# Head logits of depth 64 in a two-block transformer kernel: zero-padded queries over 128 partitions in place of products over half of the partitions

## The chip, the cores and the metric

The kernel runs on one core of one Trainium2 chip, as one launch. The metric is the device time of a launch in microseconds. Three runs of the kernel before the change took 1594.09, 1598.08 and 1592.15 us (median 1594.09). Times of single instructions below come from one profiled execution.

## The reference

The input is 256 tokens of 1024 features. Two blocks follow each other, each with two layers, all in float32.

- First block, per layer: RMS norm, one wide projection, then three mixers side by side: a gated delta rule with 4 heads, an MLA attention with 8 heads, and a gated linear recurrence. Their outputs are gated, joined and projected back.
- Second block, per layer: a feed-forward of 2816 hidden units, a mixer, a second feed-forward. The mixer joins a memory attention (4 heads of 64 dimensions over 256 memory tokens) with a recurrence (layer 0) or with a forgetting attention of 12 heads of 64 dimensions (layer 1, called fox).

Three attentions form logits with a depth of 64. In MLA a head's depth is 128 + 64: the 64 rotary dimensions of the query against one rotary key that all heads share.

```
qf = concat([q_nope (128), q_pe (64)]);  kf = concat([k_nope (128), k_pe (64, same for all heads)])
logits = einsum('bhqd,bhkd->bhqk', qf, kf) * 192**-0.5          # causal, 8 heads, both layers
logits = einsum('bhqd,bhkd->bhqk', rms(q), rms(k)) * 64**-0.5   # memory: 4 heads, both layers
logits = q.k / sqrt(64) + D_t - D_s                              # fox: 12 heads, causal, one layer
```

## The kernel before

Activations are kept with features on the 128 partitions and 256 tokens along a row. Weights stream from DRAM in chunks of 1 MB; ScalarE writes a rounded part `wh` of a chunk and VectorE the remainder `wl`, both in float32r. A linear layer is three TensorE products per 128 x 128 weight tile (`mm3`: high-high, high-low, low-high), with 256 columns each, into PSUM tiles called `acc` (4 banks). The attentions work in plain float32 with PSUM tiles called `mix` (4 banks). The trace shows two TensorE passes for every float32 product, and one for a float32r product; "pass" is used for one such MATMUL below.

Two heads of depth 64 share a tile of 128 partitions: the even head on partitions 0 to 63, the odd one on 64 to 127. The logits of a head multiply one half of the query tile with the same half of the key tile (`half = slice(64 * g, 64 * g + 64)`), so TensorE uses 64 of its rows:

- `mla_pair` (line 1243): per head g and block b of 128 queries, one product of depth 128 starts a PSUM group and the rotary product of depth 64 ends it: `matmul(ps[:, :n], qp[half, q], kpe[half, :n], start=False, stop=True)`. `kpe` holds the shared rotary key twice, on both halves. `qp` is formed from a PSUM tile: VectorE shuffles it and multiplies by the cosine, GpSimd multiplies the shuffled copy by the sine and adds both. The last of these, the GpSimd addition, releases the product. There are 4 pairs in each of two layers: 32 products, half of them with 128 key columns and half with 256.
- `mem_attn` (line 1470): `matmul(ps, q[half, g, t], self.km[l][half, g, :], start=True, stop=True)`, 8 products of 256 columns in each of two layers.
- `fox` (line 1678): the same form, 24 products, half with 128 and half with 256 columns.

`qheads` (line 1442) makes the queries of the last two: token-major projection, sums of squares per head, the scale `r` (a power on GpSimd), four transposes into one `mix` tile, and one ScalarE copy with the gain per feature (`features`). VectorE reads the logits from PSUM together with `r`.

The order of the instructions is not the written one. `trace` records every call; `Order.schedule` then simulates the five engines with nominal costs, lags and tile slots, and each engine in turn takes one of its ready instructions by urgency (the recording order for TensorE; for others the first TensorE instruction that needs them). `Order.issue` (line 543) emits the result, so every instruction of the trace stands under line 543. Each engine executes its list in order.

Of the kernel before, what the change touches and what calls it, by code (L numbers as in the profile page):

```python
# [13 lines left out]
ALU = mybir.AluOpType  # L14
# [7 lines left out]
FF = 22  # hidden tiles of a feed-forward  # L22
# tile sizes (columns of 4 bytes) and their slots
SLOTS = {"raw": (2048, 3), "wh": (1024, 3), "wl": (1024, 3), "s1": (256, 20), "s2": (512, 48), "s3": (384, 12),
         "col": (24, 56)}
# order of the 64 rope dimensions: partners lie 16 lanes apart in a quadrant of 32
# [3 lines left out]
# ---------------------------------------------------------------- host layout  # L30
# [3 lines left out]
def _pack(W, chunks):  # L34
    """(first k tile, k tiles, columns) -> flat; each chunk lies [128, k tiles, columns]"""
    out = []
    for k0, kt, cols in chunks:
        w = W[k0 * P:(k0 + kt) * P][:, cols]
        out.append(w.reshape(kt, P, -1).transpose(1, 0, 2).reshape(-1))
    return np.concatenate(out)  # L40
# [46 lines left out]
# order of the 8 tiles of 128 that the second block's output products sum over: four that are ready early, then the rest  # L87
# [27 lines left out]
def gu_pack(G, U):  # L115
    w = np.stack([G.reshape(8, P, FF, P), U.reshape(8, P, FF, P)], axis=3)  # [k, p, j, 2, f]
    return np.ascontiguousarray(w.transpose(2, 1, 0, 3, 4)).reshape(-1)
# [6 lines left out]
# columns of the parameter tile: name -> (offset, columns)  # L124
# [17 lines left out]
def prm_pack(i):  # L142
# [6 lines left out]
    def taps(w):  # [4, C] -> [128, C/128 * 4]  # L149
        return w.reshape(4, -1, P).transpose(2, 1, 0).reshape(P, -1)  # L150
# [33 lines left out]
# constants that depend on shapes alone  # L184
# [76 lines left out]
# ---------------------------------------------------------------- instruction order  # L261
# The kernel below is traced first; then each engine's instructions are put in an order that keeps the engines busy
# (a list scheduling over the traced dependences with the engines' nominal costs), and issued in that order.
ENG = ("tensor", "scalar", "vector", "gpsimd", "sync")
# how much later than the earliest of its ready instructions an engine may start a more urgent one
SLACK = {"tensor": 0.0, "scalar": 150.0, "vector": 40.0, "gpsimd": 100.0, "sync": 0.0}
PATIENCE = 400  # how far an instruction may fall behind its place in the tracing order
# free slots of a tag below which tiles are given out in tracing order only
RESERVE = {"s1": 6, "s2": 10, "s3": 4, "col": 16, "raw": 3, "wh": 3, "wl": 3, "mix": 2, "acc": 1}
# from the end of an instruction on one engine to the start of a dependent one on another  # L270
# [19 lines left out]
class Tracer:  # L290
    """stands for one engine: notes its instructions instead of issuing them"""
# [8 lines left out]
class Order:  # L300
# [10 lines left out]
    # ---- tracing  # L311
# [42 lines left out]
    def touch(self, op, r, w):  # L354
# [3 lines left out]
        if h is None:  # L358
            h = self.hist[name] = ([], [])  # writes, reads
            self.tile[name] = (t.tag, t.bufs or t.tag_meta.bufs)  # L360
            self.first.append(name)
            self.uses[name] = 0
# [66 lines left out]
    # ---- scheduling  # L429
    def schedule(self):  # L430
        """each engine in turn takes, among the instructions that could start within its slack, the first traced; tiles
        get slots in tracing order, or past it while more than the tag's reserve is free"""
# [8 lines left out]
        # urgency: the tracing order for TensorE; for the others, the first TensorE instruction that needs the result  # L441
# [104 lines left out]
# ---------------------------------------------------------------- kernel  # L546
class Kern:
    def __init__(self, ctx, tc, aps):
# [20 lines left out]
        # scratch in DRAM: blocks of the delta rule's triangles, their inverses (zero outside the diagonal blocks)  # L569
# [6 lines left out]
    def start(self):  # L576
        """the first loads in the order of their use, and TensorE kept busy meanwhile, so that its clock is up"""
# [39 lines left out]
    # ---- tiles: few sizes, so that a slot serves every stage  # L617
# [52 lines left out]
    # ---- weights: packed chunks streamed from DRAM in order, split exactly into two float32r parts  # L670
# [19 lines left out]
    def mm3(self, out, a, b, start, stop):  # L690
        """a: stationary parts, b: moving parts"""
# [16 lines left out]
    def unit(self, out, w, X, k0=0, first=True, last=True):  # L708
        """out[features, tokens] += w^T X over w's k tiles"""
# [5 lines left out]
    def proj(self, raw, X, sink):  # L715
        """the 128-column units of raw (one or two): sink(n, psum [128, n, 256])"""
# [6 lines left out]
    def proj_tok(self, raw, X, sink):  # L723
        """token-major: sink(token block, psum [128 tokens, columns])"""
# [17 lines left out]
    # ---- token statistics  # L742
# [4 lines left out]
    def colsum(self, ps, sq, rhs=None):  # L747
        """ps[:, b] = sum over partitions of sq[:, tokens of block b]"""
# [5 lines left out]
    def bcast(self, col):  # L754
        """col [128 tokens, 2] -> [128, 256], the same in every partition"""
# [13 lines left out]
    # ---- a stage's operand: the residual times its gain in float32r parts, sums of squares on the way  # L769
# [38 lines left out]
    def feed(self, j, ps, scale, stages):  # L808
        """x tile j += scale * ps, and on to the next stages"""
# [8 lines left out]
    # ---- feed-forward  # L818
# [26 lines left out]
    # ---- small pieces  # L845
# [6 lines left out]
    def silu2(self, ps, rb):  # L852
        """2 silu(ps * rb) for psum [128, n, 256]"""
# [8 lines left out]
    def softplus(self, x):  # L862
        """max(x, 0) + log1p(exp(-|x|)) for a few columns"""
# [7 lines left out]
        V.tensor_tensor(t[1], t[1], t[2], ALU.mult)      # z  # L871
        V.tensor_tensor(t[2], t[1], t[1], ALU.mult)      # z^2
# [12 lines left out]
    def conv(self, out, x, w, bias=None):  # L885
        """causal depthwise convolution of 4 taps along the tokens"""
# [8 lines left out]
    def softmax_t(self, z, mi, out):  # L895
        """z [128 queries, keys] = -logits, mi = their row minimum: out[key block] (psum) = P^T"""
# [10 lines left out]
    # ---- first block  # L907
    def gdn_scalars(self, l, raw, st):
        """rope key, write strength beta and log decay"""
# [27 lines left out]
    def gdn_proj(self, l, hp, kind, raw, st, gp):  # L937
        """keys, queries or values (kind 0, 1, 2) of heads 2hp, 2hp+1: convolution and 2 silu; sums of squares per token"""
# [25 lines left out]
    def gdn_rows(self, hp, gp, beta, gd):  # L964
        """rows k k^T and k q^T with the decays between their tokens: the diagonal blocks and the one beside them"""
# [52 lines left out]
    # DRAM scratch of 8 (head, block) squares of 128, the last rows padded so that all 16 x 16 diagonal blocks are equidistant  # L1018
# [6 lines left out]
    def gdn_inverse16(self):  # L1025
        """inverses of the 16 x 16 diagonal blocks (unit upper triangular) of four heads, one block a partition"""
        nc, V = self.nc, self.nc.vector

        def v(t, e, r, c):
            """the e x e blocks at (r, c) of the 2e x 2e diagonal blocks"""  # L1030
# [30 lines left out]
    def gdn_out(self, hp, gp):  # L1061
        """the rest of the inverses, values through the triangle, outputs [128 tokens, 2, 128] per head and their scales"""
# [3 lines left out]
        for h in range(2):  # L1066
            tu = self.s2((P, 2, 2, P))  # [block, T and its transpose U]
# [3 lines left out]
        for h in range(2):  # L1071
# [9 lines left out]
            need = [slice(0, 64), slice(64, 96)]  # T is needed there only  # L1081
# [55 lines left out]
    def rowsq(self, ps, out):  # L1137
        """out[:, b] = sums of squares of psum [128 tokens, 2 blocks of 128]"""
# [5 lines left out]
    def out_t(self, o, rr, gain, gate):  # L1144
        """token-major o [128, 2, 128] times its token scales, features first, times gain and gate, split"""
# [10 lines left out]
    def lru_pair(self, l, tp, raw, st, lw, hb):  # L1156
# [3 lines left out]
        def sink(n, ps):  # L1160
            xr = self.scaled(ps, st["rb"])
            for g in range(2):
# [8 lines left out]
                # twice the sigmoid, accurate where it is small: (1 + tanh |z/2|) exp(min(z, 0))  # L1171
# [11 lines left out]
        # -1 / (1 + t): (1 + e^-2x) / 2 and a Newton step  # L1183
# [9 lines left out]
    def mla_q(self, l, raw, st, mq, t0):  # L1193
        """tiles t0, ... of the query latent"""
# [12 lines left out]
    def mla_qr(self, mq, st):  # L1207
        """logits' scale per query: 192^-1/2 rsqrt(mean + eps / r^2), negated"""
# [22 lines left out]
    def lat_r(self, sq, n, st):  # L1231
        """rsqrt(mean + eps / r^2): the norm of a latent that still lacks its input's factor r"""
# [10 lines left out]
    def mla_pair(self, l, hp, raw, st, mq, rq, kvl, kpe, mixed):  # L1243
# [19 lines left out]
        G.tensor_tensor(qp, qp, sw, ALU.add)  # L1263
# [555 lines left out]
```

## Time and profile before

| | |
|---|---|
| timed runs | 1594.09 us median, 1592.15 to 1598.08 |
| span of the profiled execution | 1588.5 us, 5.6 us under the median; the page gives no other time of that execution |
| TensorE matmuls busy | 1569.5 us (99%), 12712 passes |
| VectorE, ScalarE, GpSimd busy | 1183.2 us (74%), 836.4 us (53%), 191.8 us (12%) |
| DMA | 46.9% of 16 engines' span |

A matmul's busy time in the trace includes time in the pipeline, so neighbouring passes overlap: a pass listed with 285 ns starts 120 ns after the one before it. What a pass costs is read from the distance of starts. In a merged row "x2" the start is that of its first instruction. A row names the rows and columns of the array as `64*128` (rows * columns) before the shape of the moving operand.

### The profile page before, as it was taken

The page shows a single profiled execution, that of the slowest core. Times are in us where ns is not written, and L with a number is a line of the kernel's source. Part 1 is how long each engine was busy: PE and PEld are TensorE (multiplying, and loading weights), DVE is VectorE, ACT ScalarE, POOL GpSimd, SP SyncE. Part 2 cuts the span into 40 slices and gives each one's busy share as a digit, 9 for nine tenths or more (in the row PEclk, how much of TensorE's full clock was granted, in tenths as well). Part 3 has the DMA queues.
Part 4 walks back from the last instruction along what each step waited for, and adds up shares of the span by engine and source line. Part 5 has one row for each costly group of instructions (what it writes and reads, how often), then busy time and mean ns, then how long its engine had stood idle before and what let it go on. Part 6 is the DMA issues. An engine that isn't in the chain of part 4 may idle for free.

```text
span 1588.5 us, 31207 instructions
## 1 busy us (share of the span) xinstructions
PE 1569.5 (99%) x12712; PEld 1520.3 (96%) x12712; DVE 1183.2 (74%) x2249; ACT 836.4 (53%) x1508; POOL 191.8 (12%) x196
## 2 busy tenths in 40 slices
PE   8999999999999999999999999999999999999999
PEld 8988999988989999999999999999999998999999
DVE  8987968996987677756888777665777666777753
ACT  5467745547765544445445444555444456654442
POOL 2301002311114100002102000021000321110000
PEclk9999999999999999999999999999999999999999
DMA  8343445343435455454334555544555743355553
GB/s 283 118 140 107 171 140 179 119 143 107 163 133 186 160 186 184 175 185 147 123 117 159 186 186 173 185 176 162 184 186 175 244 145 107 121 173 186 179 173 126
DMA packets 54598, 257.82 MB, mean 162 GB/s; under 512 B 11308, under 2 KB 21688, under 8 KB 27576
## 3 DMA queue, kind: packets, MB, share of 16 engines
q1 hardware_dynamic: 54456, 255.85, 46.9%
q8 instruction: 99, 1.62, 0.4%
q14 instruction: 43, 0.35, 0.1%
HBM read 252.39 MB, written 3.43 MB: 161 GB/s over the span
## 4 chain that ended last, share of the span: by engine, by line
PE 85%; DVE 8%; POOL 2%; issue 2%; ACT 1%; DMA 1%; SPq 0%; POOLq 0%; DVEq 0%; ACTq 0%
PE acc L543 74%; PE mix L543 11%; DVE s L543 5%; DVE wl L543 2%; POOL col L543 1%; POOL s L543 1%; DVE col L543 1%; ACT s L543 1%; ACT wh L543 0%; DMA s<-tri_out 0%; DMA tri_out<-s 0%; DMA prm<-in_prm_dram 0%; SPq L543 0%; DVE x L543 0%; ACT L543 0%
## 5 line engine op out<-in xcount | busy, mean ns | idle before, releaser
L543 PE MATMUL acc<-s,wh 128*128 128x256 f32 x6720 | 1237.5, 285 | 0.0
L543 PEld LDWEIGHTS acc<-s,wh 128*128 128x128 f32 x6720 | 1051.8, 192 | 6.9 <-issue 4.6
L543 PE MATMUL acc<-s,wl 128*128 128x256 f32 x3360 | 957.1, 285 | 1.0 <-DVE wl L543 1.0
L543 ACT ACTIVATE wh<-raw 128x1024 fp32r<-128x1024 f32 (+1 forms) x470 | 489.1, 1041 | 574.9 <-PE acc L543 410.2
L543 DVE TENSOR_TENSOR wl<-raw,wh 128x1024 fp32r<-128x1024 f32 (+1 forms) x470 | 571.4, 1216 | 241.2 <-ACT wh L543 238.8
L543 PEld LDWEIGHTS acc<-s,wl 128*128 128x128 f32 x3360 | 644.9, 192 | 2.4 <-DVE wl L543 1.4
L543 PE MATMUL mix<-s,s 128*128 128x128 f32 (+7 forms) x1072 | 162.4, 291 | 5.7 <-DVE col L543 2.4
L543 POOL TENSOR_TENSOR s<-s,s 128x256 f32<-128x256 f32 x75 | 92.8, 1240 | 597.4 <-ACT s L543 596.2
L543 PEld LDWEIGHTS mix<-s,s 128*128 128x128 f32 (+5 forms) x1072 | 119.0, 168 | 34.8 <-issue 9.1
L543 ACT ACTIVATE s<-s 128x256 fp32r<-128x256 f32 (+3 forms) x311 | 134.1, 439 | 27.0 <-DVE s L543 25.3
L543 DVE TENSOR_TENSOR s<-s,s 128x256 fp32r<-128x256 f32 (+6 forms) x302 | 128.8, 436 | 13.5 <-ACT s L543 8.1
L543 PE MATMUL acc<-wh,s 128*128 128x256 f32 x640 | 126.5, 290 | 0.0
L543 DVE TENSOR_TENSOR s<-acc,s 128x512 f32<-128x512 f32 (+1 forms) x134 | 91.9, 686 | 44.2 <-PE acc L543 43.1
L543 PEld LDWEIGHTS acc<-wh,s 128*128 128x128 f32 x640 | 103.7, 194 | 2.3 <-issue 1.6
L543 PE MATMUL acc<-wl,s 128*128 128x256 f32 x320 | 92.5, 289 | 0.0
L543 ACT ACTIVATE s<-mix 32x64 f32<-32x64 f32 (+6 forms) x208 | 65.2, 327 | 50.2 <-PE mix L543 47.5
L543 DVE SCALAR_TENSOR_TENSOR s<-s,s 128x256 f32<-128x256 f32 (+2 forms) x168 | 81.8, 493 | 5.0 <-ACT s L543 4.8
L543 POOL TENSOR_TENSOR col<-col,mhalf 128x2 f32<-128x2 f32 (+2 forms) x31 | 44.7, 1442 | 228.8 <-DVE col L543 228.8
L543 POOL TENSOR_TENSOR s<-s,cst 128x256 f32<-128x256 f32 x36 | 33.6, 946 | 311.9 <-DMA s<-rows 161.3
L543 PEld LDWEIGHTS acc<-wl,s 128*128 128x128 f32 x320 | 62.1, 194 | 1.0 <-issue 1.0
L543 DVE SCALAR_TENSOR_TENSOR x<-acc,x 128x256 f32<-128x256 f32 x96 | 39.7, 419 | 29.2 <-PE acc L543 29.1
L543 PE MATMUL mix<-cst,s 128*128 128x128 f32 (+2 forms) x338 | 57.2, 267 | 3.7 <-DVE s L543 1.7
(94 smaller groups left out, 733.0 us busy)
## 6 DMA issues: line engine op xcount, KB each, us to landing
raw<-in_gu_dram SPq DMA_DIRECT2D x88, 1024.0 KB, 4.8
raw<-in_win_dram SPq DMA_DIRECT2D x36, 1024.0 KB, 5.0
raw<-in_dn_dram SPq DMA_DIRECT2D x32, 1024.0 KB, 4.8
raw<-in_wo_dram SPq DMA_DIRECT2D x24, 1024.0 KB, 4.8
raw<-in_wina_dram SPq DMA_DIRECT2D x13, 1024.0 KB, 4.8
raw<-in_dn_dram SPq DMA_DIRECT2D x16, 768.0 KB, 4.2
raw<-in_winb_dram SPq DMA_DIRECT2D x7, 1024.0 KB, 4.8
raw<-in_wkv_dram SPq DMA_DIRECT2D x6, 1024.0 KB, 4.8
```

Of the source, the lines that this page charges most:

```text
L543: getattr(getattr(self.nc, op.eng), op.fn)(*op.args, **op.kw)
```

## The change

The three logits no longer cut the operands in halves. The query tile is stored twice, each copy with zeros in place of the other head, and the product runs over all 128 partitions. In `mla_pair` two VectorE multiplications by a 0/1 column (`hsel`, a constant that was there before) write the copies. In `qheads` the gain is multiplied by the same column, and the PSUM tile of the transposes is copied twice. `features` is cut in two for that. The file of the changed kernel also has comments and docstrings removed; the line numbers of `issue` stay.

```diff
@@ mla_pair
         G.tensor_tensor(qp, qp, sw, ALU.add)
+        qz = self.s2()
+        for g in range(2):
+            V.tensor_scalar(qz[:, g, :], qp, self.c("hsel")[:, g:g + 1], None, ALU.mult)
...
-            half = slice(64 * g, 64 * g + 64)
...
-                nc.tensor.matmul(ps[:, :n], qp[half, q], kpe[half, :n], start=False, stop=True)
+                nc.tensor.matmul(ps[:, :n], qz[:, g, q], kpe[:, :n], start=False, stop=True)
@@ qheads, features
-        q = self.s2()
-        self.features(q, qt, gain)
+        pt = self.features_ps(qt)
+        q = []
+        for h in range(2):
+            gh = self.col(1)
+            V.tensor_tensor(gh, gain, self.c("hsel")[:, h:h + 1], ALU.mult)
+            q.append(self.s2())
+            nc.scalar.activation(q[h], pt, AF.Copy, scale=gh)
         return q, r
@@ mem_attn
-                    nc.tensor.matmul(ps, q[half, g, t], self.km[l][half, g, :], start=True, stop=True)
+                    nc.tensor.matmul(ps, q[h][:, g, t], self.km[l][:, g, :], start=True, stop=True)
@@ fox
-                        nc.tensor.matmul(ps, q[half, g, b * P:(b + 1) * P], self.ksh[c][half, g, :n],
+                        nc.tensor.matmul(ps, q[h][:, g, b * P:(b + 1) * P], self.ksh[c][:, g, :n],
                                          start=True, stop=True)
```

The planner runs again over the whole program. Two places show what it makes of the MLA pairs. TensorE, third pair of the first layer, before: `mix_524`, `529`, `539`, `544` are the logits of (head 0, block 0), (0, 1), (1, 0), (1, 1); `s2_506` with `s2_505` are keys and queries of depth 128, `s1_184` is the rotary key and `s1_507` the rotary query.

```order
L543 MATMUL acc_522_600<-wh_517_595,s2_133_209 128x256
L543 MATMUL mix_524_602<-s2_506_584,s2_505_583 128x128 [waits Activation_49]
L543 MATMUL mix_524_602<-s1_184_260,s1_507_585 128x128 [waits Pool_49]
L543 MATMUL mix_529_607<-s2_506_584,s2_505_583 128x256
L543 MATMUL mix_529_607<-s1_184_260,s1_507_585 128x256
L543 MATMUL mix_539_617<-s2_506_584,s2_505_583 128x128
L543 MATMUL mix_539_617<-s1_184_260,s1_507_585 128x128
```

The same place after the change, where `mix_527`, `532`, `542` are the first three logits and `s2_518` is the tile of the two padded queries:

```order
L543 MATMUL acc_525_603<-wh_520_598,s2_133_209 128x256
L543 MATMUL mix_527_605<-s2_508_586,s2_507_585 128x128 [waits Activation_49]
L543 MATMUL mix_532_610<-s2_508_586,s2_507_585 128x256
L543 MATMUL mix_527_605<-s1_184_260,s2_518_596 128x128 [waits DVE_49]
L543 MATMUL mix_532_610<-s1_184_260,s2_518_596 128x256
L543 MATMUL mix_542_620<-s2_508_586,s2_507_585 128x128
L543 MATMUL mix_542_620<-s1_184_260,s2_518_596 128x128 [waits DVE_49]
```

The rotary product waits for VectorE where it waited for GpSimd, and the 256-column product of block 1 has moved in front of it. VectorE at the same place after the change; `s1_509` is the rotary query, which GpSimd completes between the second row and the fifth, and `wl` tiles are weight remainders:

```order
L543 STREAM_SHUFFLE s1_517_595<-acc_514_592 128x256 [waits PE_49]
L543 TENSOR_TENSOR s1_509_587<-acc_514_592,cst_66 128x256
L543 TENSOR_TENSOR wl_561_639<-raw_556_634,wh_560_638 128x1024 [waits Activation_49]
L543 SCALAR_TENSOR_TENSOR s1_485_563<-s2_320_398,s2_481_559 128x256
L543 TENSOR_SCALAR s2_518_596<-s1_509_587,cst_66 128x256 [waits Pool_49]
L543 TENSOR_SCALAR s2_518_596<-s1_509_587,cst_66 128x256
L543 SCALAR_TENSOR_TENSOR s2_493_571<-s2_494_572,s2_493_571 128x512
```

The two `TENSOR_SCALAR` rows are new in VectorE's list, and the first of them waits for GpSimd with the rest of the list behind it.

## Rows read from the trace of the kernel before

**Rows 1.** Page, part 1: busy time and share of the span by engine.
```profile
PE 1569.5 (99%) x12712; PEld 1520.3 (96%) x12712; DVE 1183.2 (74%) x2249; ACT 836.4 (53%) x1508; POOL 191.8 (12%) x196
```
**Rows 2.** Page, part 4: the chain that ended last, by engine.
```profile
PE 85%; DVE 8%; POOL 2%; issue 2%; ACT 1%; DMA 1%; SPq 0%; POOLq 0%; DVEq 0%; ACTq 0%
```
**Rows 3.** Groups of TensorE by shape: count | busy us, mean ns | idle before.
```profile
L543 PE MATMUL mix<-s,s 64*128 64x256 f32 x88 | 24.5, 426 | 2.4 <-DVE col L543 2.4
L543 PE MATMUL mix<-s,s 64*128 64x128 f32 x56 | 12.5, 329 | 2.7 <-POOL s L543 2.1 <-DVE s L543 0.5
```
**Rows 4.** TensorE in order of time, depth 128 only: start, duration, what, [idle before].
```profile
54.42 0.59 PE L543 MATMUL mix<-s 128*128 128x256 f32 x2
54.66 0.47 PE L543 MATMUL acc<-s,wl 128*128 128x256 f32 x1
54.97 0.40 PE L543 MATMUL acc<-s,wh 128*128 128x256 f32 x2
...
130.80 0.39 PE L543 MATMUL mix<-s,s 128*128 128x128 f32 x2
130.94 0.36 PE L543 MATMUL acc<-s,wh 128*128 128x256 f32 x1
131.15 0.28 PE L543 MATMUL acc<-s,wl 128*128 128x256 f32 x1
```
**Rows 5.** The same of an MLA pair with all sixteen logits passes in one run.
```profile
388.87 4.14 PE L543 MATMUL mix<-s,s 128*128 128x128 f32 x16
392.94 0.51 PE L543 MATMUL acc<-s,wh 128*128 128x256 f32 x2
393.28 0.29 PE L543 MATMUL acc<-s,wl 128*128 128x256 f32 x1
```
**Rows 6.** The same of the last third of fox: begin and end of its logits.
```profile
1362.22 0.28 PE L543 MATMUL acc<-s,wl 128*128 128x256 f32 x1
1362.43 0.93 PE L543 MATMUL mix<-s,s 64*128 64x128 f32 x8
...
1366.92 0.50 PE L543 MATMUL acc<-s,wh 128*128 128x256 f32 x2
1367.26 0.28 PE L543 MATMUL acc<-s,wl 128*128 128x256 f32 x1
```
**Rows 7.** The same of the memory attention, layer 0, and GpSimd's power there.
```profile
739.18 2.58 POOL L543 TENSOR_TENSOR col<-col,mhalf 128x8 f32<-128x8 f32 x1 [4.64 <-DVE col L543]
739.88 1.14 PE L543 MATMUL mix<-s,s 64*128 64x256 f32 x8
740.95 0.39 PE L543 MATMUL acc<-s,wh 128*128 128x256 f32 x1
742.66 1.97 PE L543 MATMUL mix<-s,s 64*128 64x256 f32 x8 [1.20 <-DVE col L543]
744.56 0.39 PE L543 MATMUL acc<-s,wh 128*128 128x256 f32 x1
```
**Rows 8.** GpSimd's rotary addition and the first rotary product in two pairs.
```profile
83.61 2.98 POOL L543 TENSOR_TENSOR s<-s,s 128x256 f32<-128x256 f32 x1
86.65 0.49 PE L543 MATMUL mix<-s,s 64*128 64x128 f32 x2 [1.12 <-POOL s L543]
...
438.02 1.59 POOL L543 TENSOR_TENSOR s<-s,s 128x256 f32<-128x256 f32 x1
439.66 5.43 PE L543 MATMUL mix<-s,s 64*128 64x128 f32 x14 [0.84 <-POOL s L543]
```
**Rows 9.** Groups nearest to what is added, and those that wait for weight remainders.
```profile
L543 DVE TENSOR_SCALAR s<-s,col 128x256 f32<-128x256 f32 x56 | 19.3, 359 | 0.2
L543 ACT ACTIVATE s<-mix,prm 128x512 f32<-128x512 f32 x10 | 6.8, 680 | 4.8 <-PE mix L543 4.8
L543 PE MATMUL acc<-s,wl 128*128 128x256 f32 x3360 | 957.1, 285 | 1.0 <-DVE wl L543 1.0
```
**Rows 10.** A stretch: length, busy (instructions) of PE, PEld, DVE, ACT, POOL, granted clock, DMA, GB/s.
```profile
441.50:448.30 6.80, 6.80 (x23) 5.05 (x24) 5.37 (x22) 3.60 (x13) 0.00 (x0) 0.50 0.66 251
```

More of the change, by code (lines that the diff above doesn't have):

```diff
@@ L1457, in qheads, with features_ps @@
         V.tensor_scalar(r, r, -0.125, None, ALU.mult)
-        q = self.s2()
-        self.features(q, qt, gain)
+        pt = self.features_ps(qt)
[5 more added lines that the diff above has]
+            nc.scalar.activation(q[h], pt, AF.Copy, scale=gh)
         return q, r
     def features(self, out, kt, gain):
+        self.nc.scalar.activation(out, self.features_ps(kt), AF.Copy, scale=gain)
+    def features_ps(self, kt):
         pt = self.mix().rearrange("p (g t) -> p g t", g=2)
@@ L1467, in features @@
                 self.transpose(pt[:, g, b * P:(b + 1) * P], kt[:, b, g * P:(g + 1) * P])
-        self.nc.scalar.activation(out, pt, AF.Copy, scale=gain)
+        return pt
     def mem_attn(self, l, raw, st, mixed):
@@ L1476, in mem_attn @@
             for h in range(2):
-                half = slice(64 * h, 64 * h + 64)
                 pt = self.mix().rearrange("p (k t) -> p k t", k=2)
@@ L1698, in fox @@
                 for h in range(2):
-                    half = slice(64 * h, 64 * h + 64)
                     m = self.fox_bias(2 * tl + h)
```

## The prediction

> **What bounds the kernel now.** I read the page's busy times first. TensorE is busy 99% of the span, VectorE 74%, ScalarE 53% [rows 1]. Busy overlaps between neighbouring passes, so this alone does not say that TensorE sets the end. The chain of waits does: 85% of it lies on TensorE and 8% on VectorE [rows 2]. So the question is what TensorE's list costs, pass by pass, and where it waits. The groups by shape give the passes that the change touches: 88 of 256 columns and 56 of 128 columns use 64 rows of the array [rows 3], that is 144 passes or 72 products. Their mean duration is modelled and cannot be used as a price. The price is read from the timeline, as distance between starts.
>
> **The price of a pass over all rows.** Take a run of float32 passes that `acc` passes follow, from its first start to the start of the second `acc` row. An `acc` pass takes 0.12 us: in [rows 5] the first two stand in one row at 392.94 and the third starts at 393.28, while the second starts 0.12 before the third, at 393.16. Two 256-column passes over 128 rows take 54.97 - 54.42 = 0.55 us, less 0.12 for the first `acc` pass leaves 0.43, so 0.215 each. Two 128-column passes take 131.15 - 130.80 = 0.35, less 0.12, so 0.115 each [rows 4].
>
> **The price of a pass over 64 rows.** The MLA pair of [rows 5] has 16 passes: eight of depth 128 and eight of depth 64, in turn, half with 128 and half with 256 columns. From 388.87 to 393.16 they take 4.29 us. Sixteen passes over 128 rows would take 8 x 0.215 + 8 x 0.115 + 0.12 = 2.76 us. The difference is 1.53 us for four products of depth 64, or 0.38 us each. No wait stands in these rows, so it is the array itself: a product over 64 rows between products over 128 rows loses time at its start, between its two passes and at its end.
>
> The places differ, so I price each.
>
> - MLA: 32 products of the kind of [rows 5], 32 x 0.38 = 12.2 us less.
> - Fox: [rows 6] runs from 1362.22 to the second `acc` pass at 1367.26 - 0.12 = 1367.14, 4.92 us. In it stand 8 `acc` passes (0.96 us) and the 16 passes of 8 products, half with 128 and half with 256 columns. At the prices over all rows this is 0.96 + 8 x 0.115 + 8 x 0.215 = 3.60 us. The difference is 1.32 us, and there are three such thirds: 4.0 us less. This is net: in the first run the two heads of a tile lie on different halves and run side by side, which is lost, but each later product stands alone between `acc` passes, which pays.
> - Memory attention: here the halves do run side by side. The first eight passes take 740.95 - 739.88 = 1.07 us to the first `acc` row [rows 7], against 7 x 0.215 + 0.03 = 1.53 us over all rows: about 0.5 us longer in each of two layers. What hides it is the wait behind it: TensorE stands 1.20 us until VectorE frees PSUM banks, and VectorE waits for the scale `r`, whose power ends on GpSimd at 739.18 + 2.58 = 741.76. None of that depends on the products. Without this cover it would cost 1.0 us. The second eight take 744.56 - 742.66 = 1.90 us to the first `acc` row against 1.53, 0.37 us longer; but banks that VectorE frees one by one may set the pace there. Bounds 0 and 0.4 us a layer; I take 0.15, nearer to zero since VectorE's reads are not shortened. 0.3 us less in both.
>
> Together 12.2 + 4.0 + 0.3 = 16.5 us.
>
> **What is added.** VectorE gets two products with a 0/1 column per MLA pair, 16 in all, at 0.36 us by the nearest group (5.8 us), and ten of one column (at most 0.36 each, 3.6 us). ScalarE gets a second copy of a PSUM tile with a gain, five of 0.68 us (3.4 us) [rows 9]. Both engines have room (26% and 47% idle), and TensorE waited only 1.0 us in all in front of the largest group that needs VectorE's weight remainders [rows 9]. I take their work as hidden behind TensorE's passes; if all of it were on the path it would cost 12.8 us.
>
> The second ScalarE copy holds back the odd head by 0.68 us. In front of it TensorE now has the even head's two products: 0.23 + 0.43 = 0.66 us in fox, 0.86 in the memory attention. So 0 to 0.1 us each; I take 0.
>
> The new wait in MLA is the one to look at. Before, GpSimd's addition released the product 0.06 us after its end (83.61 + 2.98 = 86.59, product at 86.65 [rows 8]). Now a VectorE product of 0.36 us and another hop of 0.06 us lie between: 0.42 us later. The planner has put other passes in front. In the pair of the first place shown in the order it is a 256-column product of two passes, 0.43 us, which covers the 0.42. In the first pair of the kernel it is one `acc` pass of 0.12, so its present wait of 1.12 us [rows 8] grows by 0.3. In the pair at 439.66, which waits 0.84 us now, three more products of depth 128 (2 x 0.115 + 4 x 0.215 = 1.09 us) come first, so that wait falls by 1.09 - 0.42 = 0.67. The sum over the pairs is near nothing; bounds: 2.0 us less (both present waits of [rows 8] gone), 8 x (0.42 + 0.36) = 6.2 us more (every pair exposed, and the second head's VectorE product too). I take 0, as the pairs worked out lie on both sides of it.
>
> Behind the waiting VectorE product stand weight remainders and the reads of the logits. They start later by what GpSimd is late; TensorE takes the remainders from tiles written ahead, and the 1.0 us of [rows 9] says that this lead has held.
>
> **The sum.** 1588.5 - 16.5 = 1572.0 us of span. The span is 5.6 us under the median of the timed runs, and I carry that over: 1577.6 us, 1.0% faster.
>
> **Rivals.**
>
> 1. *The halves cost nothing now, so nothing is won.* The Trainium skill, "TensorE: Matmul & The Clock Gate", in "Why this matters for your kernels", says that a small-depth product takes as long as one over the full depth and that products on distinct row groups run concurrently; by it the halves are to be kept. As a mechanism here: no gain in MLA and single fox products, and the loss of the side-by-side runs, up to 1.0 us where the cover in [rows 7] fails, 1594.1 + 1.0 = 1595.1 us. For it: those runs are real, as the 1.07 us for eight passes shows. Against it: the 1.53 us of [rows 5], where the half products stand alone.
> 2. *VectorE becomes the wait.* The first new product in each MLA pair holds VectorE's list until GpSimd is done, and the remainders behind it come late. GpSimd's addition takes 1.59 to 2.98 us [rows 8]; if TensorE lost all of it and both products (0.72 us) in every pair, that is 8 x 2.31 = 18.5 to 8 x 3.70 = 29.6 us, against 16.5 won: 1577.6 + 18.5 = 1596.1 to 1607.2 us. It decides from 16.5 / 8 = 2.1 us a pair. For it: the wait is really put in VectorE's list. Against it: the lead of the remainders, and the covers worked out above.
> 3. *The new order gives part of it back.* The planner moves the whole program, on nominal costs. A new wait of about 1 us can bring the clock down: after the wait before 439.66 the granted clock is 0.50, the lower of the two levels (1.2 GHz), from 441.5 to 448.3 [rows 8, 10], which doubles the time of what is done in it and so costs 6.8 / 2 = 3.4 us. Two more such falls and 3 us of scattered waits: 1577.6 + 9.8 = 1587.4 us.
> 4. *More than the sum.* The wait at 439.66 shrinks, and the fall behind it does not come: 1577.6 - 3.4 = 1574.2 us, or with one other fall gone too 1570.8 us.
>
> **How the numbers follow.** Forecast 1577.6 us, chance 0.58. Rival 4 0.18. Rival 3 0.15. Rival 1 0.04. Rival 2 0.05. 0.5% (8.0 us) is about what a measurement of this kernel can tell from no change, so "faster" is below 1586.1 us. It takes the forecast, rival 4 and two thirds of rival 3: 0.86. "Same" takes the rest of rival 3, rival 1 and a little of rival 2: 0.10. "Slower" (above 1602.1 us) is the heavy end of rival 2: 0.04. The range reaches on the low side to rival 4 with both falls gone and 2 us of present waits gone, 1569; on the high side to rival 3 at 1587.4 with the runs' own spread, 1588. It leaves out rivals 1 and 2 and the tails of the others.
>
> **What would show it.** In the profile after: no TensorE group with 64 rows and 128 columns; the groups with 128 rows larger by 88 and 56 passes. An MLA run of 16 logits passes at about 2.76 us to the second `acc` row in place of 4.29. A third of fox about 1.3 us shorter. The memory attention: the first eight passes at about 1.53 us to the next `acc` row, and the wait behind them shorter by about 0.5 us. VectorE with 16 new products of 128x256 near 0.36 us. The prediction is wrong if the 16-pass run stays above 4 us (rival 1), if TensorE's waits for VectorE's remainders grow from 1.0 us to tens (rival 2), or if more stretches at a granted clock of 0.50 eat the gain (rival 3).

## The result, and the profile after

| | before | changed |
|---|---|---|
| median of the runs side by side, us | 1593.12 (1588.29 to 1598.08) | 1569.26 (1567.44 to 1570.9) |
| ratio | | 0.9854 (95% interval 0.9831 to 0.9877) |
| span of the profiled execution, us | 1588.5 | 1569.1 |

The changed kernel is 1.5% faster, 23.9 us by the medians. The forecast was 1577.6 us, so the direction held, and 8.3 us came on top of it. The result lies at the low end of the range that was given (1569 to 1588).

The page first: busy times, then the chain of work that ended last, to be laid beside [rows 1, 2].

```profile
PE 1551.4 (99%) x12712; PEld 1519.7 (97%) x12712; DVE 1184.0 (75%) x2275; ACT 837.6 (53%) x1513; POOL 190.0 (12%) x196
...
PE 87%; DVE 8%; POOL 2%; issue 2%; ACT 1%; DMA 1%; SPq 0%; DVEq 0%; POOLq 0%; ACTq 0%
```

TensorE has as many passes as before and 18.1 us less busy time. VectorE has 26 instructions more and ScalarE five, and their busy times hardly rise (0.8 and 1.2 us). TensorE still makes up the chain.

The groups by shape answer to [rows 3, 9].

```profile
L543 PE MATMUL acc<-s,wl 128*128 128x256 f32 x3360 | 957.8, 285 | 1.0 <-DVE wl L543 1.0
...
L543 PE MATMUL mix<-s,s 128*128 128x128 f32 x472 | 77.5, 281 | 2.2 <-DVE s L543 1.9
L543 PE MATMUL mix<-s,s 128*128 128x256 f32 x240 | 67.8, 391 | 2.1 <-DVE col L543 1.7 <-ACT s L543 0.4
...
L543 DVE TENSOR_SCALAR s<-s,cst 128x256 f32<-128x256 f32 x16 | 5.0, 344 | 2.8 <-POOL s L543 2.8
```

No group has 64 rows and 128 columns any more. The groups over all rows were 416 and 152 passes and have grown by the 56 and 88. The 16 selection products of VectorE take 0.344 us each, and VectorE stood 2.8 us in all in front of them, waiting for GpSimd. The wait for the weight remainders `wl` is 1.0 us, as before.

An MLA pair with sixteen logits passes in one run, to be read beside [rows 5] (start, duration, what).

```profile
384.46 2.79 PE L543 MATMUL mix<-s,s 128*128 128x128 f32 x16
386.89 0.47 PE L543 MATMUL acc<-s,wl 128*128 128x256 f32 x1
387.20 0.40 PE L543 MATMUL acc<-s,wh 128*128 128x256 f32 x2
```

To the start of the second `acc` pass it is 387.20 - 384.46 = 2.74 us, where it was 4.29. The last third of fox, beside [rows 6]:

```profile
1344.10 0.28 PE L543 MATMUL acc<-s,wl 128*128 128x256 f32 x1
1344.22 1.70 PE L543 MATMUL mix<-s,s 128*128 128x128 f32 x10
...
1347.41 0.59 PE L543 MATMUL acc<-s,wh 128*128 128x256 f32 x2
1347.84 0.28 PE L543 MATMUL acc<-s,wl 128*128 128x256 f32 x1
```

From 1344.10 to 1347.84 - 0.12 it is 3.62 us, where it was 4.92. The memory attention of layer 0, beside [rows 7]:

```profile
727.01 2.58 POOL L543 TENSOR_TENSOR col<-col,mhalf 128x8 f32<-128x8 f32 x1 [4.63 <-DVE col L543]
...
727.62 1.89 PE L543 MATMUL mix<-s,s 128*128 128x256 f32 x8
...
729.16 0.47 PE L543 MATMUL acc<-s,wh 128*128 128x256 f32 x1
...
730.49 1.99 PE L543 MATMUL mix<-s,s 128*128 128x256 f32 x8 [0.74 <-DVE col L543]
...
732.13 0.59 PE L543 MATMUL acc<-s,wh 128*128 128x256 f32 x2
```

The first eight passes take 1.54 us to the next `acc` pass (1.07 before). The wait behind them is 0.74 us (1.20), so it gives back what they lost. The second eight take 1.64 us (1.90).

### Time and clock

Each run is listed with its span and its mean granted clock, and this explains most of the scatter: 24 runs of the kernel before lie between 1580.8 us of span at a clock of 0.998 and 1595.5 us at 0.987. Over nine runs of the changed kernel a straight line gives 1.3 us for each 0.001 of clock. The table takes this off each run, and gives the median of what is left. Its last column is worked out from the one profile of each kernel: the span less half of the stretches with a granted clock of 0.50, in which the expectations below are told. The experiments named in it are told below. At equal clock the executions of one kernel still scatter by 0.3 to 1.7 us (standard deviation), so differences of about 1 us in this column say nothing.

| | runs | mean span | mean clock | span at a clock of 1.000 | profile: span less half its low clock |
|---|---|---|---|---|---|
| before | 24 | 1588.7 | 0.9917 | 1577.7 | 1574.9 |
| changed | 9 | 1568.6 | 0.9948 | 1561.5 | 1560.2 |
| half rows in the new order | 5 | 1582.4 | 0.9922 | 1572.2 | 1570.7 |
| full rows in the old order | 4 | 1573.2 | 0.9945 | 1566.5 | 1564.5 |
| MLA alone | 4 | 1573.8 | 0.9945 | 1566.6 | 1566.2 |
| rotary key padded | 4 | 1573.2 | 0.9942 | 1565.5 | 1565.1 |
| the same, planner told | 4 | 1569.3 | 0.9940 | 1561.5 | 1560.5 |
| changed, planner told | 4 | 1569.2 | 0.9970 | 1565.1 | 1563.9 |
| all keys padded, planner told | 5 | 1572.3 | 0.9910 | 1560.3 | 1555.1 |
| before, planner told | 1 | 1582.2 | 0.9900 | 1569.2 | 1566.4 |

So the mean span fell by 20.1 us: 16.2 at equal clock, and 4.0 (0.0031 of clock) since TensorE was at the lower level for less time. The clocks of single executions scatter by 0.003 in either kernel, so the 4.0 us are known to about 3 us (95%). Among the kernels that were run side by side in one set, the two with half rows have mean clocks of 0.9909 (before) and 0.9922, and the three with full rows in MLA 0.9942 to 0.9945, in the old order and in the new. So this part seems to go with the rows and not with the order; what links them is not shown. One execution of the changed kernel was granted 1.000 throughout; its span is 1562.4 us, beside the 1561.5 of the table.

### The profile page after: what moved, and what is told of

The parts are those of the page before. It is cut to its first block, busy times and chain, and to the rows that moved or that the text cites. A ratio compares the mean times of both kernels' runs of the same rounds, so it can differ in the third digit from the quotient of the medians.

```text
span 1569.1 us, 31237 instructions
## 1 busy us (share of the span) xinstructions
PE 1551.4 (99%) x12712; PEld 1519.7 (97%) x12712; DVE 1184.0 (75%) x2275; ACT 837.6 (53%) x1513; POOL 190.0 (12%) x196
## 4 chain that ended last, share of the span: by engine, by line
PE 87%; DVE 8%; POOL 2%; issue 2%; ACT 1%; DMA 1%; SPq 0%; DVEq 0%; POOLq 0%; ACTq 0%
PE acc L543 76%; PE mix L543 10%; DVE s L543 5%; DVE wl L543 2%; POOL col L543 1%; ACT s L543 1%; DVE col L543 1%; POOL s L543 1%; DMA s<-tri_in 0%; ACT wh L543 0%; DMA x<-in_x_dram 0%; DVE x L543 0%; SPq L543 0%; DVEq L543 0%; POOLq L543 0%
## 5 line engine op out<-in xcount | busy, mean ns | idle before, releaser
L543 PE MATMUL mix<-s,s 128*128 128x128 f32 (+5 forms) x1072 | 152.7, 284 | 4.3 <-DVE s L543 1.9
L543 PEld LDWEIGHTS mix<-s,s 128*128 128x128 f32 (+4 forms) x1072 | 120.6, 169 | 22.3 <-DVE s L543 4.5
L543 DVE TENSOR_TENSOR s<-s,s 128x256 fp32r<-128x256 f32 (+6 forms) x302 | 129.3, 438 | 11.2 <-ACT s L543 5.8
L543 ACT ACTIVATE s<-mix 128x128 f32<-128x128 f32 (+6 forms) x208 | 65.0, 327 | 43.1 <-PE mix L543 40.5
```

The source lines that it names most:

```text
L543: getattr(getattr(self.nc, op.eng), op.fn)(*op.args, **op.kw)
```

## The experiments

Theory: a product over 64 rows loses time among products over 128 rows, and the change takes that loss away. Rivals: the gain comes from the new order of the program, or from the clock.

**Rows and order apart.** Two kernels separate them. In one, the changed kernel keeps each instruction where it is, and only the operands of the logits are cut to halves again:

```diff
-nc.tensor.matmul(ps[:, :n], qz[:, g, q], kpe[:, :n], start=False, stop=True)
+nc.tensor.matmul(ps[:, :n], qz[64 * g:64 * g + 64, g, q], kpe[64 * g:64 * g + 64, :n], start=False, stop=True)
```

(and so in the memory attention and fox).

> The changed kernel with its padded queries, its extra VectorE and ScalarE work and its instruction order kept (every engine's list is the same), only the logits products go back to 64 rows, each on the half that holds its head. Theory (the array price): the drains come back, 12.2 us in MLA and 4.0 in fox, so 14 to 18 us slower than the changed kernel (1569.3), 1583 to 1587 us, and the 16 passes of an MLA pair in one run take about 4.3 us again instead of about 2.75. Rival (the new order and its waits made the gain): it stays within 4 us of the changed kernel. Rival (the clock made it): slower only if stretches at a granted clock of 0.50 come back.

In the other, the kernel before keeps its order, and its operands lose the halves:

```diff
-nc.tensor.matmul(ps[:, :n], qp[half, q], kpe[half, :n], start=False, stop=True)
+nc.tensor.matmul(ps[:, :n], qp[:, q], kpe[:, :n], start=False, stop=True)
```

> The kernel before with its order kept on every engine and nothing added; only the logits products read all 128 rows of the unpadded tiles. It leaves out the separation of the two heads of a tile (their logits are added up). Theory (the array price): 14 to 18 us faster than before (1593.1), 1575 to 1579 us, and up to 24 us faster if the stretches at a granted clock of 0.50 behind those products go as well. Rival (order): within 4 us of before. If the added VectorE and ScalarE work of the change costs anything, this one is faster than the changed kernel by that much; hidden work means equal within 3 us.

Half rows in the new order: 1584.43 us, ratio to before 0.9956 (0.9933 to 0.9978). Full rows in the old order: 1575.35 us, 0.9903 (0.9880 to 0.9927). Both times lie where they were expected, but the clock has a part in that (0.9922 and 0.9945). At equal clock the rows bring 1577.7 - 1566.5 = 11.2 us in the old order and 1572.2 - 1561.5 = 10.7 in the new one. The order brings 5.5 with half rows and 5.0 with full rows. The sums agree, though the rows come to their 11 us in different ways in the two orders, as the next part shows. Where the lists of both orders agree again, at 500 us, the new order is ahead by 4.4 us with half rows and 3.9 with full ones, and from there on it gains nothing more. The same run of sixteen passes, first with half rows in the new order:

```profile
390.67 4.14 PE L543 MATMUL mix<-s,s 128*128 128x128 f32 x16
394.74 0.39 PE L543 MATMUL acc<-s,wl 128*128 128x256 f32 x1
394.96 0.41 PE L543 MATMUL acc<-s,wh 128*128 128x256 f32 x2
```

and with full rows in the old order:

```profile
386.80 2.79 PE L543 MATMUL mix<-s,s 128*128 128x128 f32 x16
389.23 0.59 PE L543 MATMUL acc<-s,wh 128*128 128x256 f32 x2
389.66 0.28 PE L543 MATMUL acc<-s,wl 128*128 128x256 f32 x1
```

That is 394.96 - 390.67 = 4.29 us against 389.66 - 0.12 - 386.80 = 2.74: it goes with the rows, whatever the order. The Trainium skill, "TensorEngine Tiling (Array Packing)", "Key Properties", says that a change of the tiling mode drains TensorE; it gives no size. The trace agrees that there is a loss: 1.55 us for four half products among full ones. Taken singly from the trace, the starts in the run of [rows 5] show more than a loss at each change. From the third pass on, every start comes about 0.1 us later than over all rows, also between the two passes of one product, where the tiling stays: 0.20 to 0.21 us between passes of 128 columns, where the full rows have 0.11, and 0.31 to 0.32 with 256 columns, where they have 0.22. So the full products in the run lose too.

**Where the rest of the MLA gain went.** Eight pairs at 1.53 us should bring 12.2 us. The kernel before and the one with full rows execute the same list, so their passes can be laid side by side one by one; stretches at a granted clock of 0.50 are counted at half their length there. By 500 us, behind the last MLA pair, the full rows are ahead by 6.5 us only. The missing part shows as waits that the old order did not have, or had shorter. Full rows in the old order, in the second and the last pair ([...] is idle time before, and what ended it):

```profile
145.56 0.29 PE L543 MATMUL acc<-s,wl 128*128 128x256 f32 x1
146.35 1.58 PE L543 MATMUL mix<-s,s 128*128 128x128 f32 x8 [0.50 <-DVE col L543]
```
```profile
456.33 0.58 PE L543 MATMUL acc<-s,wh 128*128 128x256 f32 x2
457.21 0.33 PE L543 MATMUL mix<-cst,s 128*128 128x128 f32 x1 [0.30 <-DVE s L543]
```

In the kernel before, the first place has no wait:

```profile
142.15 0.28 PE L543 MATMUL acc<-s,wl 128*128 128x256 f32 x1
142.26 2.06 PE L543 MATMUL mix<-s,s 128*128 128x128 f32 x8
```

TensorE now arrives 0.78 us earlier at the second half of the logits (1.55 us from the first half's start to the `acc` pass in front, where it was 2.33), and VectorE has not freed the banks: 0.67 us more to wait. At the transposes of the last pair it arrives 1.5 us earlier, and 0.46 are given back. There are nine such places with 0.25 to 0.67 us, 3.4 in all; the other 2.3 us lie in steps too small to assign. In the new order the last pair has more `acc` passes between the logits and the first transpose (`mix<-cst,s`):

```profile
449.43 3.11 PE L543 MATMUL mix<-s,s 128*128 128x128 f32 x16
452.19 0.59 PE L543 MATMUL acc<-s,wh 128*128 128x256 f32 x2
...
454.17 0.27 PE L543 MATMUL mix<-cst,s 128*128 128x128 f32 x1
```

There are 1.98 us from the first `acc` pass to the transpose, and no wait. In the old order two `acc` passes stand there, 0.24 us of work.

Side by side, half rows in the new order against the changed kernel, the rows bring 6.05 us in MLA, as little as in the old order, but for another reason. Only one place gives back more than 0.2 us. In five of the eight pairs the planner has put rotary products next to each other: two of the four in three pairs, all four in the last two. Half products in one run lose nothing. Half rows in the new order, in the last pair but one:

```profile
441.95 1.18 PE L543 MATMUL mix<-s,s 64*128 64x128 f32 x8 [1.03 <-DVE s L543]
443.06 0.51 PE L543 MATMUL acc<-s,wh 128*128 128x256 f32 x2
```

The changed kernel at the same place:

```profile
434.18 1.58 PE L543 MATMUL mix<-s,s 128*128 128x128 f32 x8 [1.03 <-DVE s L543]
435.40 0.59 PE L543 MATMUL acc<-s,wh 128*128 128x256 f32 x2
```

That is 1.11 us with half rows and 1.22 with full ones, behind the same wait. With half rows, the new order gains 2.2 of its 4.4 us between 430 and 461 us, where these two pairs stand.

**MLA alone.** Only the hunk of `mla_pair` on the kernel before.

> Only the MLA part of the change: padded rotary queries, 32 products over all rows; memory attention and fox as before. Theory: 12.2 us of the gain is here, so 1578 to 1583 us by the sum from 1593.1; the rest (4 to 8 us, with the stretches of low clock at the memory attention and fox) stays. Rival (the gain sits in fox and the memory attention through the clock): less than 8 us faster than before.

1575.31 us, ratio 0.9907 (0.9887 to 0.9928), faster than the 1578 to 1583 expected; at equal clock 11.1 us less than before. Its TensorE list is that of the changed kernel, pass by pass, so the order's 5.5 us are in it, and MLA's rows have the other 5.6 (1572.2 - 1566.6), not 12.2. Fox and memory attention bring the 5.1 that are left to the changed kernel (3.8 side by side in the old order).

**The zeros in the key.** If the selection products of VectorE cost anything, they can go: the shared rotary key is padded once a layer, and the product waits for GpSimd again.

```diff
-qz = self.s2()
-for g in range(2):
-    V.tensor_scalar(qz[:, g, :], qp, self.c("hsel")[:, g:g + 1], None, ALU.mult)
...
-nc.tensor.matmul(ps[:, :n], qz[:, g, q], kpe[:, :n], start=False, stop=True)
+nc.tensor.matmul(ps[:, :n], qp[:, q], kpe[:, g, :n], start=False, stop=True)
```

> The changed kernel, but in MLA the zeros stand in two copies of the rotary key (made once a layer) instead of two copies of the rotary query (made once a pair): 16 VectorE products fewer, and the rotary product waits for GpSimd again, not for VectorE. Theory (hidden work, short waits): the waits in front of the rotary products shrink by up to 0.42 us in each of 8 pairs, 0 to 3 us faster than the changed kernel: 1566 to 1569 us. Rival (the wait on VectorE holds up its list and costs more than seen at TensorE): 5 us or more faster.

1574.86 us, ratio 0.9901 (0.9879 to 0.9924): a miss. Without the selection products it is 4.0 us slower than the changed kernel at equal clock, and within 1.0 us of full rows in the old order. Its TensorE list is the old one but for two of the 12712 passes. So what the removal took away is the new order, and the ScalarE copies that this kernel still has cost nothing beyond the scatter. Of the selection products no run shows the cost apart from the order.

**Is the order's gain a matter of what the planner believes?** A selection product in the planner's list makes it expect the logits later and put other passes in front. If so, its price for GpSimd, 0.69 us for one addition of 256 columns by the formula below, where [rows 8] show 1.59 to 2.98, would do the same when raised:

```diff
-return 147 + 2.11 * n
+return 147 + 4.2 * n
```

It was raised in the kernel with the padded key, in the changed kernel, and in the kernel before.

> The kernel with padded rotary keys, with one number of the planner changed: a GpSimd product of 256 columns is planned with 1.22 us where it was 0.69 (the trace has 1.2 to 1.6). No instruction is added or removed, only the order. Theory (the new order won 4 us because the VectorE product made the planner expect the logits later, and so put other passes in front of what waits): the order now fills the waits without that product, 3 to 6 us faster than the padded key alone, 1568 to 1572 us, level with the changed kernel. Rival (the order's part was an accident of the reshuffling): no gain over 1574.9, or a loss.

> The changed kernel with the same number of the planner changed, 1.22 us for a GpSimd product of 256 columns. Theory: the waits that are left in front of the rotary products (0.28 to 1.2 us in four pairs) shrink, 0 to 4 us faster than the changed kernel. Rival (accident of the order): anything within 3 us on either side.

> The kernel before with half rows, the planner told 1.22 us for a GpSimd product of 256 columns; only the order changes. Theory (order and array price add up): by the order's part of the padded key it gains about 4 us, span less half of the stretches at 0.50 near 1570.7 as with the new order and half rows. Rival (chance of the reshuffling): anywhere from 1568 to 1578.

The padded key then takes 1571.11 us, ratio 0.9872 (0.9844 to 0.9901), at equal clock the 1561.5 of the changed kernel. The changed kernel takes 1570.49, 0.9872 (0.9842 to 0.9902), at equal clock 3.6 us worse. The padded key came out as expected (1568 to 1572). From the changed kernel 0 to 4 us were expected; as timed beside itself it gains 1.3 (1571.79, told below), but by its clock of 0.9970 alone. The kernel before, in one run, gains 8.5 us at equal clock with its halves kept, where about 4 were expected. Its TensorE list is that of the padded key with the raised price but for 36 passes, so the rows bring 7.7 us (1569.2 - 1561.5) in this order, where they brought 11 in the others. So the one number moves the time by -4.0, +3.6 and -8.5 us. This speaks for chance: each new list finds other gaps. The six kernels with full rows in all three attentions have four TensorE lists: the old one (1566.5, and 1565.5 with the padded key), the new one (1561.5), that of the raised price without selection products (1561.5, and 1560.3 below) and that of the raised price with them (1565.1). The changed kernel is near the good end, the old order at the bad one. That the planner's later date for the logits helps in itself is not shown.

**All keys padded.** Zeros in the keys of the memory attention and fox as well, with the raised price.

> Zeros in the keys everywhere (rotary key once a layer, memory keys once a layer, fox keys once a tile, all made long before their use) and the planner told 1.22 us for a GpSimd product of 256 columns. The second ScalarE copy leaves the path of the queries. Theory: products over all rows as in the changed kernel, so the span less half of the stretches at 0.50 is 1559 to 1565 us, in the band of the other versions with padded tiles (1560.2 to 1565.1), and timed 1568 to 1575. Rival (the late copy of the odd head's queries costs): 1 us or more below 1560.2.

1572.07 us, ratio 0.9887 (0.9853 to 0.9921). It has the lowest span at equal clock, 1560.3 us, but not by more than the scatter, and the lowest mean clock, 0.9910, as one of its five executions had 0.983 and the others 0.993. The profile was taken of that one, with 54.7 us of low clock: 1555.1 us less half of it is under the expected 1559 to 1565, on the rival's side. Half is too much to take off, as the last part shows, which weighs most here, so whether the second ScalarE copy costs 1 us is left open. No version is clearly faster than the changed kernel.

**The two kernels again,** to see which low-clock stretches recur.

> The changed kernel once more, unaltered, beside the others of this set. Theory on the clock: the time of one execution moves with the stretches at a granted clock of 0.50, so this profile may have another set of them than the first (17.1 us at 0.50 there), while the span less half of those stretches repeats within 1 us (1560.6). Timed 1567 to 1571 us. Rival: the stretches repeat as well, as they belong to the order.

> The kernel before once more, unaltered, for its profile. Theory on the clock: other stretches at 0.50 than in the first profile (27.3 us there), the span less half of them again 1574.9 within 1 us. Rival: the same stretches and a span of 1588.5 within 1 us.

> The kernel before a third time, for its stretches at a granted clock of 0.50 (27.3 and 31.4 us so far). Theory: the span less half of them is 1574.7 within 0.5 us again, whatever the stretches are.

> The changed kernel a third time, for its stretches at a granted clock of 0.50 (17.8 and 28.6 us so far). Theory: the span less half of them is 1560.5 within 0.5 us again.

The changed kernel timed again: 1571.79 us, ratio 0.9859 (0.9815 to 0.9903), just above the 1567 to 1571 expected. The single runs: before 1592.47 and 1589.69 us, changed 1572.99. Less half of their low clock the spans are 1574.6 and 1580.2 us for before (the second is taken up at the end), 1560.7 and 1561.0 for the changed kernel. Stretches (length, busy us and instructions of PE, PEld, DVE, ACT, POOL; granted clock; DMA share; GB/s), first of two executions of the kernel before:

```profile
356.10:362.93 6.83, 6.83 (x49) 5.54 (x49) 5.00 (x11) 2.17 (x9) 0.00 (x0) 0.50 0.18 46
...
1305.00:1308.40 3.40, 3.40 (x15) 2.78 (x14) 2.84 (x16) 1.95 (x8) 0.00 (x0) 0.50 0.00 0
```
```profile
357.40:377.90 20.50, 20.50 (x119) 16.18 (x118) 8.43 (x19) 9.74 (x30) 0.00 (x0) 0.50 0.30 103
1347.20:1350.60 3.40, 3.40 (x16) 3.14 (x15) 1.38 (x5) 0.00 (x0) 0.00 (x0) 0.50 0.00 0
```

and of two of the changed kernel:

```profile
353.30:363.50 10.20, 9.84 (x71) 7.27 (x71) 5.70 (x10) 4.40 (x15) 0.00 (x0) 0.50 0.42 119
441.50:448.30 6.80, 6.80 (x58) 6.77 (x58) 6.48 (x14) 6.47 (x14) 0.94 (x2) 1.00 0.47 155
```
```profile
351.70:368.80 17.10, 16.74 (x108) 12.54 (x107) 9.12 (x20) 5.12 (x19) 0.00 (x0) 0.50 0.24 72
```

The one near 355 us, in the small products of the second layer's delta rule, recurs in all of them, with 7 to 20 us. The ones at 1305 and 1347 us came each in one execution alone. A single profile can't say which fall the change took away; the means over 24 and 9 runs can say that there is less low clock, 4.0 us of it.

## Why the prediction was right in direction and 8.3 us too high

**The price of the rows: right at each place.** 2.74 us for the MLA run (2.76 forecast), 3.62 us for the fox third (3.60), 1.54 us for the first eight of the memory attention (1.53), the wait behind them shorter by 0.46 us (0.5).

**The sum of the rows: too large, in the MLA term.** 16.5 us was forecast and 10.7 to 11.2 measured in one order. Side by side, pass by pass, MLA gives 6.5 us and not 12.2, fox 3.65 (4.0), the memory attention 0.17 (0.3). The step that failed is "32 products of the kind of [rows 5]", carried whole into the sum: it took MLA's passes as bound by TensorE throughout, and all 32 half products as standing alone. A pair is a chain of TensorE, VectorE and ScalarE, and where passes behind the logits had only just been covered, a shorter run of logits turned part of its gain into a new wait. And with half rows in the new order the products of five pairs stand together in part, at no loss there (1.11 us at 441.95).

**The new order: priced at 0, brought 5.** The bounds were 2.0 us less and 6.2 more, so this lies outside them. They held the present waits at two pairs and the new hops alone; the planner moved much of the list. The pairs worked out came out otherwise. The places of [rows 8], GpSimd's addition, VectorE's product, the rotary product:

```profile
84.58 1.68 POOL L543 TENSOR_TENSOR s<-s,s 128x256 f32<-128x256 f32 x1
...
86.31 0.35 DVE L543 TENSOR_SCALAR s<-s,cst 128x256 f32<-128x256 f32 x1
...
86.71 0.49 PE L543 MATMUL mix<-s,s 128*128 128x128 f32 x2
...
431.39 1.59 POOL L543 TENSOR_TENSOR s<-s,s 128x256 f32<-128x256 f32 x1
...
433.78 0.61 DVE L543 TENSOR_SCALAR s<-s,cst 128x256 f32<-128x256 f32 x2
...
434.18 1.58 PE L543 MATMUL mix<-s,s 128*128 128x128 f32 x8 [1.03 <-DVE s L543]
```

In the first pair the new step costs what was said, 86.71 - 86.26 = 0.45 us after GpSimd's end (0.42). But GpSimd took 1.68 us where it had taken 2.98, so the wait fell where a rise was forecast. In the pair that had waited 0.84 us a fall to 0.17 was forecast, and it waits 1.03. There GpSimd was done at 432.98 and VectorE began 0.80 us later; the row in front of it in its list shows why:

```profile
432.31 1.54 DVE L543 SCALAR_TENSOR_TENSOR s<-s,s 128x256 f32<-128x256 f32 x2
```

The product stood in VectorE's list behind other work. The forecast asked only what queues behind the new instruction, not what stands in front of it.

**Added work: right as far as it is shown.** The ScalarE copies cost nothing beyond the scatter on the old order of TensorE (1565.5 beside 1566.5 us). The selection products hold TensorE at single places; no run tells their cost from the gain of the order that came with them.

**From span to median: wrong.** 5.6 us was carried over as if it were fixed. Each run lists its own span, and time less span is 2.1 us on the mean for the kernel before. That is 3.5 us too much. The three runs known then were slower executions than the profiled one; by the line above that is clock, but theirs is not on record. The clock gave another 4.0, which the forecast had left to rival 4. With the parts: 1588.7 - 5.5 (order) - 10.7 (rows) - 4.0 (clock) + 1.9 (time over span) = 1570.4 us, beside the mean of 1570.5 of the changed kernel's nine runs. Against that mean the forecast is 7.1 us high, 3.5 + 4.0 less 0.3 for a sum of 16.5 in place of 16.2, to 0.1. The forecast's own 16.5 us at equal clock was right as a number (16.2) by luck: two errors cancelled.

**The rivals.** Rival 1 (the halves cost nothing) falls with 4.29 against 2.74 us in either order. The rule that a product of small depth takes as long as a full one (the Trainium skill, "TensorE: Matmul & The Clock Gate", "Why this matters for your kernels") does not hold for a lone half product between full ones: 0.39 us more each. Rival 2 falls too: VectorE's 2.8 us of waiting for GpSimd and 0.344 us a product reach the path at single places, such as 434.18. Rival 3 (the order gives part back) had the wrong sign, and its tie between a wait and the clock did not hold: behind the 1.03 us at 434.18 the granted clock stays 1.00 from 441.5 to 448.3, where it was 0.50 in [rows 10]. Nor did it hold for the kernel before: in its second and third execution the same wait of 0.84 us stands in front of 446.01 and 444.26, and the granted clock is 1.00 from 430 to 460 us in both. Rival 4 (more than the sum) came true in size, by less low clock in the mean.

## What to carry to other kernels

Price a pass by the distance of starts, in the company that it keeps: a half product that stands alone between full ones can cost more than a full one with zeros. Then ask how far ahead of the next engine each shortened run was; what it gains beyond that lead can come back as a wait. Where a planner sets the order, take several orders before a few us are put down to a change, compare the lists to see which kernels share an order, and compare runs at equal clock.

## What the runs showed that was not expected

Low clock does not double every pass. In the changed kernel's second profile, at 0.50, three `acc` passes take 0.64 us (18.68 to 19.32 in the rows at the end), 0.213 each, and 0.12 at full clock: such a stretch costs 0.44 of its length, not the half that rival 3 and the pass-by-pass comparison took.

The clock's record can be incomplete. The third execution of the kernel before shows 1.00 where its passes keep the spacing of the lower level:

```profile
10.50:20.50 10.00, 9.08 (x41) 8.76 (x42) 7.91 (x21) 4.30 (x9) 1.62 (x1) 1.00 1.00 365
```
```profile
18.69 0.41 PE L543 MATMUL acc<-s,wl 128*128 128x256 f32 x1
18.91 0.63 PE L543 MATMUL acc<-s,wh 128*128 128x256 f32 x2
19.33 0.41 PE L543 MATMUL acc<-s,wl 128*128 128x256 f32 x1
```

The second execution of the changed kernel has the same spacing there with 0.50 on record:

```profile
10.40:20.60 10.20, 9.19 (x42) 8.87 (x43) 8.00 (x21) 4.12 (x9) 1.62 (x1) 0.50 1.01 357
```
```profile
18.68 0.41 PE L543 MATMUL acc<-s,wl 128*128 128x256 f32 x1
18.89 0.63 PE L543 MATMUL acc<-s,wh 128*128 128x256 f32 x2
19.32 0.41 PE L543 MATMUL acc<-s,wl 128*128 128x256 f32 x1
```

That is why the third execution of before missed its expectation (1580.2 us less half of what is on record, where 1574.7 was expected): some 10 us of low clock lack there, about 5 us of time. One more of the 24 runs lies as far off the line (1589.5 us of span at a listed 0.995).

Part of the scatter at equal clock is a wait for a DMA. In front of the delta rule's products near 345 us TensorE waits for the read-back of a scratch tile (`tri_out`): in three executions of the changed kernel not at all, 1.22 us (at 350.0) and 0.35 us (at 348.3).
